# Leads of the projection stream in branch B's three phases raised by 0.2 in a hybrid encoder kernel

## The chip, the cores and the metric

The kernel runs on one core of a Trainium2 chip. The metric is the device time of one execution in microseconds (us); smaller is better. Five engines work beside each other, each through its own instructions in their written order, and wait for each other by semaphores: PE (TensorE, matmuls and transposes, with its weight loads shown apart as PEld), DVE (VectorE), ACT (ScalarE), POOL (GpSimd) and SP (SyncE), which here issues all DMAs.

## The reference, cut to what matters

One encoder layer is applied to two independent groups of 1024 tokens, called prompt (g = 0) and sample (g = 1), with the same weights. From the normalised input `h` one wide projection gives queries, keys and values of two attention branches, their gate paths `z`, and two merge gates `ga`, `gb`.

```
proj = einsum('bsd,de->bse', h, w_in)
qa, ka, va, za, qb, kb, vb, zb, ga, gb = split(proj)
# branch A: 8 query heads on 2 key heads of 64, RMS norm and rotary on q and k
oa = gqa_attention(qa, ka, va) * silu(za)
# branch B: 4 heads; two 64-dim softmax maps per head, 128-dim values
s  = einsum('bqhmd,bkhmd->bhmqk', qblk, k) * scale
p  = softmax(s, axis=-1)
pd = p[:, :, 0] - lam * p[:, :, 1]
ob = rms_norm(einsum('bhqk,bkhe->bqhe', pd, v), subln_g) * (1 - lam_init)
ob = ob * silu(zb)
merged = sigmoid(ga) * (oa @ w_proj_a) + sigmoid(gb) * (ob @ w_proj_b)
y = x + gate * (merged @ w_out)
```

## The kernel before

**Streams of PE work.** Each group is worked off in turn. Within a group there are three kinds of work that compete for PE.

- Attention. `attention` (its steps are sorted by a fixed rule) goes through 32 units: 16 of branch A, then four for each head of branch B. A unit of branch B covers 256 queries and makes four score tiles `s` (128 queries by 1024 keys, one of the two maps). A score tile is four matmuls (L747, L748); DVE takes the row maximum (L749), ACT the exponential (L750). Once both maps of 128 queries are there, DVE joins them with the learned factor that POOL finishes (L775, L776, L790), transposes the result in blocks of 32 (L791), four DMAs put the pieces into place (L800), and about 1.4 units later eight matmuls multiply by the values (L823, tile `a`; the trace records two for each). Score tiles live in two buffers of PSUM (`ps_s`), so a tile can begin only when the exponential of the tile two before it is done.
- Projections for the next head, called here the projection stream. `qkb_gen` makes queries and keys of one head of branch B: for each of eight token tiles 24 matmuls of 256 columns (`proj_tt`, L540), then a chain: two ACT passes (L555, L556), DVE's sum and epsilon (L559, L560), on POOL the power, the norm, the gains and the rotary step (L561, L563, L681, L574, L582, L583, in the tile `row`), and a transpose on PE (L594) two token tiles later, whose result ACT and DVE split into the tiles `u` that the scores read (L596, L597). `vb_gen` makes values for two heads in the same way without the chain.
- Gate pieces. `z_gen` makes the gates `z`, `ga` and `gb`: 24 matmuls of 512 columns for a tile (L713), a tanh, and a DMA to DRAM.

Weights come by DMA into `st`, are split in two parts by ACT (L193) and POOL (L195), and live in two buffers `w` shared by projection stream and gate pieces.

**What sets the order.** `phase(k, ...)` runs phase k of a group: k = 0 and 1 in branch A, k = 2, 3 and 4 for the heads 0, 1 and 2 of branch B, in which the projections for the next head are made (in k = 3 also the values for heads 2 and 3). The last head has no such stream; it is woven with gate pieces and the first steps of the merge. `weave` gives the next turn to the stream whose done share, less its lead, is smallest:

```
s = min(live, key=lambda s: s[2] / s[1] - s[3])
...
n_att = 8 * 6 if k < 2 else 4 * 11
nz = 3 * Z_SHARE[g][k]
weave(
    (until_next(att), n_att * ATT_W[g][k], 0.0), (chain(*fs), 31 * len(fs), IN_A[g][k]),
    (islice(zs, nz), nz, Z_A[g][k]), *more,
)
```

Attention has the lead 0, the projection stream `IN_A[g][k]`, the gate pieces `Z_A[g][k]`. A lead of 0.4 means that the projection stream may be 0.4 of its length ahead of attention. The shares of gate pieces by phase (`Z_SHARE`) are fixed; besides, the end of each `qkb_gen` takes up to two gate steps before each of its last transposes (`pipelined`). The order so written is a wish: a scheduler then orders the instructions of each engine by their priority in the written order and by its own estimate of when each is ready, with attention's instructions raised by 100 places.

Of the kernel before, what the change touches and what calls it, by code (L numbers as in the profile page):

```python
# [44 lines left out]
    (1.229, 1.265, 0.9, 1.0, 0.85, 1.069),  # L45
)
IN_A = (
    (0.1, 0.05, 0.4, 0.05, -0.05, 0.1),
    (0.1, 0.05, 0.4, 0.1, 0.15, 0.55),
)  # L50
Z_A = (
    (0.15, 0.0, 0.2, -0.1, 0.0, 0.0),
# [1284 lines left out]
```

## Time and profile before

| what | value |
|---|---|
| runs before | 1917.95 us median of 3 (1914.27 to 1920.34) |
| the profiled execution's own time | 1911.4 us |
| its span, first to last instruction | 1909.6 us |
| mean granted clock of TensorE | 0.986 |
| DVE busy | 1209.3 us (63%) |
| ACT busy | 771.6 us (40%) |
| POOL busy | 666.6 us (35%) |
| branch B in the prompt group | from about 457 to 790 us |
| branch B in the sample group | from about 1360 to 1710 us |

The profile's page gives busy time by engine, the chain that ended last and the costliest groups of instructions. A window view gives busy time of each engine and the granted clock in stretches that one chooses. A timeline lists instructions in order; in square brackets stands how long the engine sat idle before one and what ended that. Busy time of PE is made from matmuls that overlap in its pipeline: a matmul of 512 columns is recorded with about 0.4 us, while the next one starts about 0.23 us after it.

### The profile page before, as it was taken

To read this page: it belongs to the slowest core of one execution; us is meant where nothing else is said; L and a number is where in the kernel's file an instruction comes from. 1 tells how busy PE (TensorE), PEld (TensorE's weight loads), DVE (VectorE), ACT (ScalarE), POOL (GpSimd) and SP (SyncE) were. 2 spreads that over 40 slices of the span, in tenths; PEclk is the share of its full clock that TensorE was granted. 3 is DMA by queue.
4 is the path that set the end of the run, shared out by engine and by line. 5 is a ranking of instruction groups with operands and counts; after the bars stand their busy time and mean duration, and the time that the engine had idled before them with its cause. 6 is when DMAs were issued, how large, how long until landed. Compare 5 with 4: busy or idle time off the path is not lost.

```text
span 1909.6 us, 29522 instructions
## 1 busy us (share of the span) xinstructions
PE 1847.3 (97%) x10398; PEld 1553.5 (81%) x10398; DVE 1209.3 (63%) x1791; ACT 771.6 (40%) x1576; POOL 666.6 (35%) x904
## 2 busy tenths in 40 slices
PE   6999999999999999999999999999999899999999
PEld 3788778888888978788888877888898798877887
DVE  5777753454876667457467787445366746674795
ACT  4545443443554444213233455344354535332241
POOL 2234511442654551221232343024474736212100
PEclk7999999999999999999999999999999999999999
DMA  9126675554443557864531567665434424586442
GB/s 320 57 84 163 186 199 159 161 151 141 111 123 104 161 152 229 281 183 156 200 107 51 146 188 196 183 182 161 138 92 115 129 70 109 163 254 211 147 126 90
DMA packets 273044, 295.04 MB, mean 155 GB/s; under 512 B 35200, under 2 KB 221696, under 8 KB 272896
## 3 DMA queue, kind: packets, MB, share of 16 engines
q1 hardware_dynamic: 272896, 293.15, 51.8%
q8 instruction: 83, 1.36, 0.3%
q14 instruction: 65, 0.53, 0.1%
HBM read 133.59 MB, written 42.01 MB: 92 GB/s over the span
## 4 chain that ended last, share of the span: by engine, by line
PE 74%; DMA 7%; DVE 6%; SPq 4%; issue 4%; POOL 3%; ACT 2%; DVEq 0%; ACTq 0%; POOLq 0%
PE f L713 20%; PE f L540 17%; PE f L985 5%; PE a L806 5%; PE s L747 5%; PE s L748 5%; PE a L823 4%; PE s L985 3%; PE f L1020 3%; SPq L800 2%; PE s L1020 2%; DMA st<-in_w_in_dram 2%; PE f L1092 2%; DVE m L749 2%; PE s L1092 1%
## 5 line engine op out<-in xcount | busy, mean ns | idle before, releaser
L713 PE MATMUL f<-u,w 128*128 128x512 f32 x2256 | 582.2, 398 | 2.7 <-POOL w L195 1.2
L713 PEld LDWEIGHTS f<-u,w 128*128 128x128 f32 x2256 | 416.5, 189 | 88.9 <-POOL w L195 2.4
L540 PE MATMUL f<-w,u 128*128 128x256 f32 x3456 | 477.8, 287 | 1.3 <-ACT w L193 0.3
L540 PEld LDWEIGHTS f<-w,u 128*128 128x128 f32 x3456 | 452.4, 192 | 22.1 <-issue 3.5
L749 DVE TENSOR_REDUCE m<-s 128x1 f32<-128x1024 f32 x256 | 310.3, 1219 | 200.0 <-PE s L748 198.0
L750 ACT ACTIVATE p<-s,m 128x1024 f32<-128x1024 f32 x256 | 285.1, 1114 | 279.0 <-DVE m L749 238.8
L195 POOL TENSOR_TENSOR w<-st,w 128x512 fp32r<-128x512 f32 x160 | 215.8, 1366 | 441.1 <-ACT w L193 424.8
L791 DVE STREAM_TRANSPOSE p<-p 128x1024 f32<-128x1024 f32 x192 | 237.6, 1241 | 58.0 <-ACT p L750 50.0
L561 POOL TENSOR_TENSOR rs<-ss,nhalf 128x4 f32<-128x4 f32 (+1 forms) x112 | 110.0, 983 | 308.7 <-DVE ss L560 271.8
L748 PE MATMUL s<-u,sw 128*128 128x512 f32 x512 | 203.8, 399 | 0.0
L193 ACT ACTIVATE w<-st 128x512 fp32r<-128x512 f32 x184 | 108.2, 627 | 98.1 <-DMA st<-in_w_in_dram 83.3
L985 PE MATMUL f<-u,w 128*128 128x512 f32 x552 | 134.8, 398 | 2.3 <-DVE u L1000 2.3
L823 PE MATMUL a<-q,u 128*128 128x256 f32 x512 | 127.0, 385 | 8.9 <-DMA q<-p 4.2
L985 PEld LDWEIGHTS f<-u,w 128*128 128x128 f32 x552 | 105.0, 192 | 24.6 <-DVE u L1000 2.5
L597 DVE TENSOR_TENSOR u<-f,u 64x256 fp32r<-64x256 f32 (+1 forms) x194 | 79.7, 411 | 71.3 <-ACT u L596 66.4
L806 PE MATMUL a<-q,u 128*64 128x256 f32 x1024 | 117.8, 382 | 2.0 <-DMA q<-p 2.0
L823 PEld LDWEIGHTS a<-q,u 128*128 128x128 f32 x512 | 95.3, 192 | 24.5 <-issue 7.6
L747 PE MATMUL s<-u 128*128 128x512 f32 x256 | 106.5, 418 | 4.9 <-ACT p L750 4.9
L748 PEld LDWEIGHTS s<-u,sw 128*128 128x128 f32 x512 | 97.2, 190 | 16.8
L790 DVE SCALAR_TENSOR_TENSOR p<-p,r,p 128x1024 f32<-128x1024 f32 x64 | 91.3, 1427 | 28.5 <-POOL r L776 26.8
L806 PEld LDWEIGHTS a<-q,u 128*64 128x64 f32 x1024 | 73.4, 137 | 40.3 <-issue 6.9
L747 PE MATMUL s<-u,u 128*128 128x512 f32 x256 | 102.9, 402 | 1.4 <-ACT p L750 1.4
(215 smaller groups left out, 2032.3 us busy)
## 6 DMA issues: line engine op xcount, KB each, us to landing
q<-p SPq DMA_DIRECT2D x768, 128.0 KB, 2.6
st<-in_w_in_dram SPq DMA_DIRECT2D x132, 256.0 KB, 3.2
zd<-ev SPq DMA_DIRECT2D x96, 256.0 KB, 2.7
sw<-u SPq DMA_DIRECT2D x256, 64.0 KB, 2.0
u<-in_w_ada_dram SPq DMA_DIRECT2D x8, 1024.0 KB, 11.4
od<-oo SPq DMA_DIRECT2D x64, 128.0 KB, 2.4
st<-in_w_in_dram SPq DMA_DIRECT2D x64, 128.0 KB, 2.7
row<-od SPq DMA_DIRECT2D x32, 256.0 KB, 2.9
```

The source lines that it names most:

```text
L195: e.tensor_tensor(out=wl, in0=st, in1=wh.bitcast(F32), op=ALU.subtract)
L540: ins = nc.tensor.matmul(ps, lt[c][:, sl], w[:, c, wi, :], start=(k == 0), stop=(k == 23))
L561: nc.gpsimd.tensor_tensor(out=rs, in0=ss, in1=nhalf[:, :nh], op=ALU.pow)
L713: ins = nc.tensor.matmul(ps, w[:, c, wi, e * P : (e + 1) * P], rt[c], start=(k == 0), stop=(k == 23),)
L747: nc.tensor.matmul(s[:, sl], q, k[:, sl], start=True, stop=False)
L748: nc.tensor.matmul(s[:, sl], sw, k[:, sl], start=False, stop=True)
L749: nc.vector.tensor_reduce(out=m, in_=s, axis=AX.X, op=ALU.max, negate=True)
L750: nc.scalar.activation(pt.rearrange("p (j c a) -> p j c a", j=4, c=8), s.rearrange("p (c a j) -> p j c a", c=8, j=4), AF.Exp, bias=m, accu ...
L791: nc.vector.transpose(pt, pt)
L806: lambda k=k, m=m: nc.tensor.matmul(acc[(LO, HI)[m]], u["v"][:, k], pT[m][:, k], start=(k == 0), stop=(k == 7))
L823: nc.tensor.matmul(acc, u["v"][:, k], pT[:, k], start=(k == 0), stop=(k == 7))
L985: nc.tensor.matmul(ps, w[:, c, wi, d * P : (d + 1) * P], o[:, oi, :], start=(k == 0), stop=(k == 11))
```

## The change

Six numbers of one table change: the lead of the projection stream in phases 2, 3 and 4 of each group goes up by 0.2. In both groups phase 2 goes from 0.4 to 0.6; phases 3 and 4 go from 0.05 and -0.05 to 0.25 and 0.15 in the prompt group, and from 0.1 and 0.15 to 0.3 and 0.35 in the sample group. No instruction is added or taken away; their order on all five engines differs from the beginning of phase 2 to the end of branch B in each group, and nowhere else.

```diff
 IN_A = (
-    (0.1, 0.05, 0.4, 0.05, -0.05, 0.1),
-    (0.1, 0.05, 0.4, 0.1, 0.15, 0.55),
+    (0.1, 0.05, 0.6, 0.25, 0.15, 0.1),
+    (0.1, 0.05, 0.6, 0.3, 0.35, 0.55),
 )
```

Three places show what becomes of it on PE.

**Place 1**, PE at the end of phase 4 of the prompt group, before: `a_7241` are the values of the last unit of head 2, `f_7103` a gate tile, `f_7192` and `f_7251` a side computation of the residual's gate (L325), `s_7185` and `s_7208` the first score tiles of head 3, `f_7114` and `f_7151` the last two transposes of its queries and keys.

```order
L594 MATMUL f_7114<-ident,row_6954 128x128 x2
L713 MATMUL f_7103<-u_329,w_7086 128x512
L713 MATMUL f_7103<-u_330,w_7086 128x512
L713 MATMUL f_7103<-u_329,w_7086 128x512 x2
L713 MATMUL f_7103<-u_330,w_7086 128x512
L713 MATMUL f_7103<-u_329,w_7086 128x512
L823 MATMUL a_7241<-q_7066,u_5989 128x256 x8
L594 MATMUL f_7151<-ident,row_7025 128x128 x2
L325 MATMUL f_7192<-u_7193,cT 32x512 x4
L835 MATMUL f_7221<-ones_c,at_7196 128x1 x2
L325 MATMUL f_7192<-u_7218,cT 32x512 x4
```

The same place on PE in the changed kernel; the last transposes and the gate tile stand ahead of these rows.

```order
L325 MATMUL f_7192<-u_7193,cT 32x512 x4
L325 MATMUL f_7192<-u_7218,cT 32x512 x4
L835 MATMUL f_7221<-ones_c,at_7196 128x1 x2
L747 MATMUL s_7185<-u_6425 128x512
L748 MATMUL s_7185<-u_6425,sw_7141 128x512
L747 MATMUL s_7208<-u_6426 128x512
L748 MATMUL s_7208<-u_6426,sw_7141 128x512
L337 MATMUL f_7244<-pick,row_7242 128x2 x4
L325 MATMUL f_7251<-u_7252,cT 32x512 x4
L325 MATMUL f_7251<-u_7272,cT 32x512 x4
L823 MATMUL a_7241<-q_7136,u_5909 128x256 x8
```

The values `a_7241` moved behind both L325 tiles, the last transposes and the second halves of two score tiles; ahead of it, 21 matmuls of the projection stream that stood after the unit's last score tile are gone, since the stream ended earlier.

**Place 2**, PE at the end of phase 2 of the sample group, before: the last token tile of head 1's queries and keys is transposed into `f_14163`, with the scores of `s_14428`, the first tile of head 1, ahead of it.

```order
L713 MATMUL f_14100<-u_9082,w_13524 128x512
L747 MATMUL s_14293<-u_12421 128x512
L748 MATMUL s_14293<-u_12421,sw_14181 128x512
L747 MATMUL s_14293<-u_12421 128x512
L748 MATMUL s_14293<-u_12421,sw_14181 128x512
L747 MATMUL s_14428<-u_13503 128x512
L748 MATMUL s_14428<-u_13503,sw_14271 128x512
L594 MATMUL f_14163<-ident,row_14066 128x128
```

In the changed kernel the same token tile is transposed into `f_14099`.

```order
L747 MATMUL s_14279<-u_12420 128x512
L748 MATMUL s_14279<-u_12420,sw_14181 128x512
L713 MATMUL f_14071<-u_9082,w_13604 128x512
L713 MATMUL f_14071<-u_9084,w_13604 128x512
L713 MATMUL f_14071<-u_9082,w_13604 128x512 x2
L713 MATMUL f_14071<-u_9084,w_13604 128x512
L713 MATMUL f_14071<-u_9082,w_13604 128x512
L594 MATMUL f_14099<-ident,row_13972 128x128
```

Between the last projection matmul of this token tile and its transpose there stood 30 gate matmuls and 14 score matmuls; now 42 gate matmuls, 16 score matmuls and the eight of a unit's values stand there.

**Place 3**, PE at the end of phase 3 of the sample group, before: three score tiles of head 1 in a row (a fourth, `s_15151`, stands just ahead of them), then a transpose of the projection stream and a gate tile.

```order
L747 MATMUL s_15239<-u_13503 128x512
L748 MATMUL s_15239<-u_13503,sw_15117 128x512
L747 MATMUL s_15239<-u_13503 128x512
L748 MATMUL s_15239<-u_13503,sw_15117 128x512
L747 MATMUL s_15254<-u_13504 128x512
L748 MATMUL s_15254<-u_13504,sw_15117 128x512
L747 MATMUL s_15254<-u_13504 128x512
L748 MATMUL s_15254<-u_13504,sw_15117 128x512
L594 MATMUL f_14824<-ident,row_14707 128x128 x2
L713 MATMUL f_14848<-u_9077,w_14831 128x512
```

The same place on PE in the changed kernel.

```order
L594 MATMUL f_14734<-ident,row_14582 128x128 x2
L823 MATMUL a_15026<-q_14703,u_11710 128x256 x8
L747 MATMUL s_15217<-u_13504 128x512
L748 MATMUL s_15217<-u_13504,sw_15011 128x512
L747 MATMUL s_15217<-u_13504 128x512
L748 MATMUL s_15217<-u_13504,sw_15011 128x512
L747 MATMUL s_15239<-u_13503 128x512
L748 MATMUL s_15239<-u_13503,sw_15195 128x512
L747 MATMUL s_15239<-u_13503 128x512
L748 MATMUL s_15239<-u_13503,sw_15195 128x512
L594 MATMUL f_14761<-ident,row_14638 128x128 x2
L713 MATMUL f_14785<-u_9077,w_14768 128x512
```

The run of four score tiles is broken up: a unit's values stand ahead of `s_15217`, and a transpose and 22 gate matmuls now stand between `s_15239` and `s_15254`.

## The prediction

> **What bounds the kernel now.** The page comes first: its opening line and its first list show which engine has no room.
>
> ```profile
> span 1909.6 us, 29522 instructions
> PE 1847.3 (97%) x10398; PEld 1553.5 (81%) x10398; DVE 1209.3 (63%) x1791; ACT 771.6 (40%) x1576; POOL 666.6 (35%) x904
> ```
>
> PE is busy for 97% of the span, and the change neither adds nor removes a matmul. A gain can only come out of PE's gaps, and a loss only from new ones. So the second view is the busy time by stretch, here the three projection phases and the last head, first of the prompt group, then of the sample group. The columns are stretch, length, busy time of PE, PEld, DVE, ACT and POOL with counts, granted clock, DMA share, GB/s.
>
> ```profile
> 470.00:530.00 60.00, 59.95 (x343) 51.99 (x340) 44.61 (x62) 32.05 (x68) 35.75 (x59) 1.00 0.37 102
> 530.00:600.00 70.00, 68.50 (x420) 61.39 (x420) 51.99 (x76) 34.70 (x75) 41.66 (x74) 1.00 0.42 117
> 600.00:682.00 82.00, 82.00 (x539) 75.55 (x538) 55.95 (x79) 37.88 (x80) 41.04 (x62) 1.00 0.51 147
> 682.00:790.00 108.00, 101.43 (x487) 81.66 (x486) 69.72 (x99) 41.26 (x78) 31.29 (x42) 0.98 0.69 212
> 1385.00:1446.00 61.00, 61.00 (x369) 54.52 (x368) 44.78 (x63) 32.34 (x67) 41.08 (x65) 1.00 0.39 105
> 1446.00:1514.00 68.00, 59.71 (x354) 51.94 (x352) 48.27 (x74) 34.66 (x74) 43.95 (x73) 0.95 0.41 112
> 1514.00:1590.00 76.00, 76.00 (x508) 70.55 (x507) 39.62 (x60) 28.11 (x60) 30.18 (x50) 1.00 0.33 91
> 1590.00:1710.00 120.00, 116.57 (x552) 97.93 (x552) 82.14 (x107) 53.65 (x102) 44.56 (x61) 0.99 0.61 180
> ```
>
> Three of the eight rows have no gap at all, a fourth has 0.05 us. What there is to win lies in three rows: 1.50, 6.57 and 8.29 us of idle PE, with the clock below 1.00 in the last two; of the 6.57, place 1 holds 3.44, and the rest stands with the final row's 3.43 in the last heads, where the order hardly changes. The third view, PE's timeline, gives each long gap and what ended it.
>
> ```profile
> 695.84 5.38 PE L823 MATMUL a<-q,u 128*128 128x256 f32 x16 [3.44 <-DMA q<-p]
> 1450.02 0.33 PE L594 MATMUL f<-ident,row 128*128 128x128 f32 x1 [2.62 <-POOL row L583]
> 1450.62 5.73 PE L713 MATMUL f<-u,w 128*128 128x512 f32 x17
> 1508.50 0.50 PE L747 MATMUL s<-u 128*128 128x512 f32 x1 [2.84 <-ACT p L750]
> 1510.42 0.63 PE L748 MATMUL s<-u,sw 128*128 128x512 f32 x1
> 1510.85 0.63 PE L747 MATMUL s<-u 128*128 128x512 f32 x1
> 1513.78 0.44 PE L594 MATMUL f<-ident,row 128*128 128x128 f32 x2 [1.88 <-POOL row L583]
> 589.73 3.61 PE L823 MATMUL a<-q,u 128*128 128x256 f32 x16
> 600.84 4.02 PE L713 MATMUL f<-u,w 128*128 128x512 f32 x17
> ```
>
> Four gaps, and behind three of them slow work: the same 16 matmuls took 5.38 us instead of 3.61, the same 17 took 5.73 instead of 4.02, and score matmuls of the same width began 0.43 us apart instead of 0.24 (4.02 / 17). So a long gap costs its length and about 1.7 us more: **3.44 + 1.77 = 5.2** (place 1), **2.62 + 1.71 = 4.3** (place 2), **2.84 + 1.88 + 8 x 0.19 = 6.2** (place 3). Together 15.7 us stand on what ends each phase: the next head's last transposes, or scores and values packed together.
>
> [...]
>
> **The change, part by part.** No instruction is new, so the terms are waits that go, waits that stay, and waits that come.
>
> *Place 1, goes nearly: -5.2 + 1.0.* The values must wait for the last score tile of their unit, its softmax and four DMAs.
>
> ```profile
> 682.70 0.39 PE L748 MATMUL s<-u,sw 128*128 128x512 f32 x1
> 683.43 1.23 DVE L749 TENSOR_REDUCE m<-s 128x1 f32<-128x1024 f32 x1
> 690.95 1.93 SPq L800 DMA_DIRECT2D q<-p  x3
> 701.36 1.07 PE L325 MATMUL f<-u,cT 128*32 128x512 f32 x8
> ```
>
> From the last score matmul's end (683.09) to the values (695.84) the need is 12.7 us. In the changed order these stand between them: 24 gate matmuls, 24 x 0.236 = 5.7 (4.02 / 17); 8 score matmuls, 1.9; the L325 tiles, four times 1.07 = 4.3; two transposes and small ones, about 1.2. That is 13.1, so the wait is just covered. It is covered by little: SP, where a load for L325 and one for `st` stand ahead of the last pieces `q`, can add delay, and the 1.07 may hold some of the half clock. Bounds for what stays are 0 and 5.2; I take 1.0, near the cover worked out.
>
> *Place 2, goes: -4.3.* The transpose waited for POOL's rotary step, and POOL for a weight split that stood between the norm and the gains of this token tile.
>
> ```profile
> 1437.02 0.39 ACT L555 ACTIVATE row<-f 128x256 f32<-128x256 f32 x1
> 1443.13 1.02 POOL L561 TENSOR_TENSOR rs<-ss,nhalf 128x4 f32<-128x4 f32 x1 [1.31 <-DVE r L775]
> 1444.44 0.61 POOL L563 TENSOR_TENSOR row<-row,rs 128x256 f32<-128x256 f32 x1
> 1446.80 1.28 POOL L195 TENSOR_TENSOR w<-st,w 128x512 fp32r<-128x512 f32 x1 [1.74 <-ACT w L193]
> 1448.03 0.73 POOL L681 TENSOR_TENSOR row<-row,gB 128x256 f32<-128x256 f32 x1
> 1449.11 0.46 POOL L582 TENSOR_TENSOR row<-row,sinB 128x32 f32<-128x32 f32 x2
> 1449.65 0.32 POOL L583 TENSOR_TENSOR row<-rc,row 128x64 f32<-128x64 f32 x1
> ```
>
> The chain took 12.95 us (1437.02 to 1449.97) against 44 matmuls of cover, some 10.4 us. The changed order has 42 x 0.236 + 16 x 0.24 + 3.6 for the values = 17.3 us of cover, 4.4 more than the chain needed. If a weight piece came that much later the wait would be back; bounds 0 and 4.3, taken as gone.
>
> *Place 3, halves: -6.2 + 3.1.* Here DVE is the slower engine for a while. Its rows from 1458 to 1515, with one stretch, and 24 projection matmuls of the chain of waits:
>
> ```profile
> L749 DVE TENSOR_REDUCE m<-s 128x1 f32<-128x1024 f32 x14 | 17.1, 1219 | 5.2 <-PE s L748 5.1
> L790 DVE SCALAR_TENSOR_TENSOR p<-p,r,p 128x1024 f32<-128x1024 f32 x6 | 8.1, 1342 | 1.4 <-POOL r L776 1.4
> L791 DVE STREAM_TRANSPOSE p<-p 128x1024 f32<-128x1024 f32 x5 | 6.2, 1240 | 0.1
> L597 DVE TENSOR_TENSOR u<-f,u 64x256 fp32r<-64x256 f32 x12 | 5.1, 422 | 1.1 <-ACT u L596 0.9
> L559 DVE TENSOR_REDUCE ss<-row 128x4 f32<-128x256 f32 x8 | 3.3, 410 | 0.9 <-ACT row L556 0.8
> 1500.00:1515.00 15.00, 10.21 (x54) 7.79 (x53) 14.10 (x20) 10.63 (x22) 13.34 (x21) 0.89 0.46 123
> 657.68 2.87 PE f L540 x24
> ```
>
> DVE worked 14.10 of 15 us at the two gaps. In the changed order the four tiles no longer stand together, but a stretch ahead of them is denser: over eight score tiles (up to `s_15217`) DVE has 8 maxima (9.8), 4 joins (5.4), 4 transposes (5.0), 8 splits (3.4), 4 sums (1.6) and about 2.2 of small work, 27.4 us; PE has 32 score matmuls (7.6), 72 projection matmuls (8.6, at 2.87 for 24), 8 for values (3.6) and about 0.9 of small ones, 20.7 us. The difference of 6.7 us is spread over eight tiles, each of which may run up to one tile late for nothing, since there are two score buffers. Bounds are 0 (all hidden) and 6.7 + 1.7 = 8.4 (all shown in one piece); I take half the old cost, 3.1.
>
> *Small waits, stay and come: +2.0.* The remaining gaps between 470 and 1515 are of this size:
>
> ```profile
> PE f L713 <- DVE ssB L837: 1.0, 1, 1.0
> PE f L594 <- POOL row L583: 0.5, 1, 0.5
> 1485.00:1500.00 15.00, 14.12 (x91) 12.61 (x90) 10.73 (x19) 8.92 (x20) 10.79 (x20) 1.00 0.52 142
> ```
>
> The first two are from the list of who waited for whom, the third is a stretch with 0.88 us idle. I leave these as they are, and add two new ones of 1.0 for bursts: in the changed order most phases begin with some 72 projection matmuls close together, so three token tiles reach POOL at once. Bounds are 0 and three waits like place 2, 13. At nothing I cost the gate pieces' new places (PE's total is the same), the earlier weight loads (their buffers come free 5 us or more of PE work ahead, as before), and SP's shifts in the last head; their cover is PE's own backlog.
>
> **Sum**: -5.2 + 1.0 - 4.3 - 6.2 + 3.1 + 2.0 = **-9.6 us**. On the profiled execution's own 1911.4 us that gives 1901.8. Its own time lies 6.5 us below the median of the runs, 1917.95; the gain is taken off the median: **1908.3 us**.
>
> **Rivals.**
>
> *DVE takes it back.* At place 3 all of the 8.4 us shows, 5.3 more than taken: -4.3, 1913.7. For it speaks DVE's 14.10 of 15; against it that before, the tiles stood closer. [...] Chance 0.22.
>
> *POOL becomes the bound, slower.* Three token tiles in a burst of 8.6 us bring POOL 3 x (1.02 + 0.61 + 0.73 + 0.46 + 0.32) = 9.4 us and a little for the cosine step, beside four weight splits of 1.28, so about 15. If the transposes, 10 to 12 us behind in PE's order, wait as at place 2 in most of the six phases, each costs 4.3. From the third such wait on, the gain is used up (3 x 4.3 = 12.9 against 11.6 without the 2.0); six make 25.8 - 11.6 = +14.2, 1932. Against it: POOL is busy for 41 of 61 us and less elsewhere, and the cover of the last transpose grew where it had waited. Chance 0.10.
>
> *All waits of these phases go*, the small ones too: -15.7 - 1.0 - 0.5 - 0.9 = -18.1, 1899.9. Chance 0.10.
>
> *It does not do what it says.* The ends of the phases were full already: the rows 600:682 and 1514:1590 have PE at 100%, so gates put there fill nothing, and the four gaps are chance meetings that reappear elsewhere at the same price. 1918. Against it: each of the three places has its own longer cover in the new order. Chance 0.08.
>
> **How the numbers follow.** Forecast 0.50, the rivals 0.22, 0.10, 0.10, 0.08. About 0.3% (5.75 us) is what a measurement of this kernel can tell from no change, so faster is below 1912.2. The forecast falls below it but for 0.05, the greater gain wholly, and 0.05 of the first rival: faster 0.45 + 0.10 + 0.05 = 0.60. Within: 0.05 + 0.17 + 0.08 = 0.30; slower 0.10. The range goes from 1897, a little under the case in which all goes, to 1921, which takes in no change and part of the slower side; it leaves out the upper part of the POOL case and a tail of the others.
>
> **What would show it.** Right: no PE gap over 2 us before the values at the end of the prompt's phase 4, none before the last transpose of the sample's phase 2, granted clock 1.00 in both; at the sample's phase 3 a few gaps of about 1 us ended by ACT. Wrong: gaps of PE ended by POOL L583 early in the phases (the slower rival), or several us ended by ACT L750 at the sample's phase 3 (the first). The forecast fails if the waits move rather than go: the same 8 and 6 us in other rows of the stretch table.

## The result, and the profile after

The kernel was compared with the one before twice; the second comparison is run e9 below.

| comparison | before | after | ratio, 95% interval |
|---|---|---|---|
| first, 5 runs and 5 | 1917.75 us (1914.27 to 1920.34) | 1905.77 us (1902.43 to 1909.83) | 0.9940 [0.9920, 0.9961] |
| second, 23 runs and 10 | 1913.41 us (1905.84 to 1923.92) | 1905.24 us (1900.65 to 1907.85) | 0.9963 [0.9949, 0.9976] |

The changed kernel is faster by 12.0 or 8.2 us. The two medians of the changed kernel agree within 0.5 us; the kernel before differs by 4.3. The profiled execution after is the run of 1905.77, against 1911.4 for that of before: between the two traces the difference is 5.6 us.

The page's first lines, as before: the same matmuls, the same busy time of PE.

```profile
span 1904.0 us, 29515 instructions
PE 1846.8 (97%) x10398; PEld 1554.6 (82%) x10398; DVE 1212.2 (64%) x1791; ACT 771.7 (41%) x1576; POOL 666.1 (35%) x904
```

Busy time by stretch, the same columns and the same eight stretches of work. Their bounds moved with the work, so the lengths differ from those before.

```profile
470.00:530.00 60.00, 60.00 (x334) 51.89 (x331) 45.18 (x64) 33.29 (x69) 36.39 (x61) 1.00 0.41 115
530.00:600.00 70.00, 68.02 (x415) 61.14 (x414) 51.53 (x75) 33.83 (x72) 39.80 (x71) 0.98 0.41 112
600.00:692.00 92.00, 91.12 (x583) 82.86 (x583) 57.99 (x83) 41.99 (x89) 50.75 (x77) 1.00 0.47 135
692.00:790.00 98.00, 94.70 (x453) 75.84 (x452) 68.06 (x91) 37.26 (x70) 23.73 (x30) 1.00 0.78 240
1385.00:1446.00 61.00, 60.22 (x361) 53.30 (x359) 47.64 (x68) 32.80 (x71) 43.54 (x71) 1.00 0.41 114
1446.00:1506.00 60.00, 55.33 (x337) 49.56 (x336) 44.54 (x66) 30.42 (x65) 42.19 (x67) 0.97 0.42 115
1506.00:1582.00 76.00, 76.00 (x511) 70.50 (x510) 44.01 (x65) 31.70 (x67) 30.53 (x56) 1.00 0.34 90
1582.00:1705.00 123.00, 118.73 (x551) 98.95 (x550) 81.83 (x105) 52.11 (x99) 42.93 (x54) 0.97 0.59 178
```

The fourth row lost 3.3 us of idle time (6.57 to 3.30): the 3.44 of place 1 go, 1.47 come (at 696.97), and the last head's own waits are 1.3 shorter. The sixth row still has 4.67 us of its 8.29: place 2 is gone, place 3 is not. PE's timeline of the changed kernel, only the rows in front of which PE sat idle in the projection phases (the row at 684.23 also shows what 16 matmuls for values take at full clock: 3.69 us, granted clock 1.00 from 684.25 to 687.90), and ahead of the last one the end of the values of the unit before it:

```profile
590.22 0.44 PE L594 MATMUL f<-ident,row 128*128 128x128 f32 x2 [1.21 <-POOL row L583]
591.30 0.67 PE L594 MATMUL f<-ident,row 128*128 128x128 f32 x2 [0.65 <-POOL row L583]
670.57 3.26 PE L823 MATMUL a<-q,u 128*128 128x256 f32 x14 [0.23 <-DMA q<-p]
684.23 3.69 PE L823 MATMUL a<-q,u 128*128 128x256 f32 x16 [0.51 <-DVE r L775]
696.97 0.33 PE L594 MATMUL f<-ident,row 128*128 128x128 f32 x1 [1.47 <-POOL row L583]
1417.74 3.69 PE L823 MATMUL a<-q,u 128*128 128x256 f32 x16 [0.78 <-DMA sw<-u]
1473.15 1.46 PE L823 MATMUL a<-q,u 128*128 128x256 f32 x6
1499.18 5.41 PE L823 MATMUL a<-q,u 128*128 128x256 f32 x16 [4.62 <-DVE oo L829]
```

The last row is the one to look at. At the end of the sample's phase 3 the values wait 4.62 us and then run 1.72 us longer than the 16 of another unit do at 684.23 (5.41 us instead of 3.69; granted clock 0.50 from 1499.35 to 1502.70), 6.3 us together. What they wait for is the copy L829, which empties the only accumulator `a` (the pool `ps_a` has one buffer). DVE's rows at that place:

```profile
1495.17 1.22 DVE L749 TENSOR_REDUCE m<-s 128x1 f32<-128x1024 f32 x1
1496.43 2.03 DVE L790 SCALAR_TENSOR_TENSOR p<-p,r,p 128x1024 f32<-128x1024 f32 x1
1498.38 0.41 DVE L559 TENSOR_REDUCE ss<-row 128x4 f32<-128x256 f32 x1
1498.71 0.41 DVE L829 COPY oo<-a 128x256 f32<-128x256 f32 x1
```

DVE has no pause in them. The copy stands in its queue behind a maximum, a join and a sum, so PE waits for work that has nothing to do with the accumulator. PE stopped at 1494.56. Of the 4.62 us from there, 0.61 pass before DVE begins the maximum of the tile that PE has just finished, 1.26 go with that maximum, 1.95 with the join, 0.33 with the sum and 0.47 with the copy. The values that the copy takes out had ended at 1474.61 already, 24.1 us before the copy began; ACT's square of the same accumulator (L828), which stands just as late in ACT's order, ran at 1495.14.

### The profile page after: what moved, and what is told of

It reads as the page before. It is cut to its first block, busy times and chain, and to the rows that moved or that the text cites. A ratio compares the mean times of both kernels' runs of the same rounds, so it can differ in the third digit from the quotient of the medians.

```text
span 1904.0 us, 29515 instructions
## 1 busy us (share of the span) xinstructions
PE 1846.8 (97%) x10398; PEld 1554.6 (82%) x10398; DVE 1212.2 (64%) x1791; ACT 771.7 (41%) x1576; POOL 666.1 (35%) x904
## 4 chain that ended last, share of the span: by engine, by line
PE 70%; DMA 8%; DVE 7%; POOL 5%; issue 4%; SPq 3%; ACT 2%; POOLq 0%; DVEq 0%; ACTq 0%
PE f L713 18%; PE f L540 16%; PE a L806 5%; PE f L985 5%; PE s L747 4%; PE s L748 4%; PE a L823 3%; PE s L985 3%; PE f L1020 3%; DMA row<-zd 2%; SPq L800 2%; PE s L1020 2%; DVE m L749 2%; PE f L1092 2%; DMA q<-p 1%
## 5 line engine op out<-in xcount | busy, mean ns | idle before, releaser
L540 PE MATMUL f<-w,u 128*128 128x256 f32 x3456 | 470.9, 287 | 1.7 <-ACT w L193 0.9
L750 ACT ACTIVATE p<-s,m 128x1024 f32<-128x1024 f32 x256 | 285.1, 1114 | 290.6 <-DVE m L749 227.8
L790 DVE SCALAR_TENSOR_TENSOR p<-p,r,p 128x1024 f32<-128x1024 f32 x64 | 89.2, 1393 | 20.6 <-POOL r L776 18.7
## 6 DMA issues: line engine op xcount, KB each, us to landing
u<-in_w_ada_dram SPq DMA_DIRECT2D x8, 1024.0 KB, 11.4
```

The source lines that it names most:

```text
L540: ins = nc.tensor.matmul(ps, lt[c][:, sl], w[:, c, wi, :], start=(k == 0), stop=(k == 23))
L750: nc.scalar.activation(pt.rearrange("p (j c a) -> p j c a", j=4, c=8), s.rearrange("p (c a j) -> p j c a", c=8, j=4), AF.Exp, bias=m, accu ...
```

## The experiments

Two questions were open: does each place win on its own, so that a larger lead is a dial to turn (theory A), or do the waits only meet by chance in each order (theory B)? And is the wait at place 3 one of DVE's load? "PE idle" below is 490 us less PE's busy time in the windows 455 to 705 and 1360 to 1600 us, which hold the projection phases; it was 13.27 us before and is 9.78 after. Each ratio is against runs of the kernel before on the same chip. PE idle is that of the one execution that was profiled; in e3, e6 and e8 it took 1913.02, 1912.79 and 1920.29 us, 6 to 9 us away from the median.

| run | leads raised by | median, us | ratio, 95% interval | PE idle, us |
|---|---|---|---|---|
| e1 | 0.2, prompt only | 1907.54 | 0.9969 [0.9957, 0.9982] | 12.27 |
| e2 | 0.2, sample only | 1908.85 | 0.9977 [0.9964, 0.9990] | 11.90 |
| e3 | 0.1 | 1920.40 | 1.0043 [1.0029, 1.0058] | 17.51 |
| e4 | 0.4 | 1934.36 | 1.0113 [1.0092, 1.0133] | 23.21 |
| e5 | 0.02 | 1930.93 | 1.0101 [1.0083, 1.0119] | 24.13 |
| e6 | 0.22 | 1906.84 | 0.9977 [0.9962, 0.9993] | 11.17 |
| e7 | 0.2, not in the sample's phase 3 | 1907.34 | 0.9980 [0.9968, 0.9992] | 14.20 |
| e8 | 0.2, copy L829 on ACT | 1911.76 | 0.9995 [0.9978, 1.0012] | 17.15 |
| e9 | 0.2, the changed kernel again | 1905.24 | 0.9963 [0.9949, 0.9976] | 10.06 |
| e10 | 0.2, joins and transposes cut | 1887.18 | 0.9860 [0.9839, 0.9882] | 3.30 |
| e11 | 0.4, joins and transposes cut | 1920.31 | 1.0038 [1.0023, 1.0052] | 18.48 |
| e12 | 0.02, joins and transposes cut | 1908.40 | 0.9969 [0.9954, 0.9984] | 14.48 |

### One group at a time (e1, e2), and the whole once more (e9)

```diff
 IN_A = (
-    (0.1, 0.05, 0.4, 0.05, -0.05, 0.1),
+    (0.1, 0.05, 0.6, 0.25, 0.15, 0.1),
     (0.1, 0.05, 0.4, 0.1, 0.15, 0.55),
 )
```

That is e1; e2 changes the second row alone, e9 both.

> Only the prompt group's three leads are raised; the sample group keeps the order of before. Theory A, each place has its own cover: the wait for the values at the prompt's phase 4 (place 1) goes and nothing else changes, so the gain is what the traces show up to the start of the sample group, 3.6 to 3.8 us, about 1914 against a kernel before of 1917.8; its PE gaps in the sample group are those of before, with 2.62 us ahead of the last transpose of phase 2 and 2.84 us among the score tiles of phase 3. Theory B, chance meetings: the gain is not tied to the group; it lies anywhere from 0 to 12 us, and gaps in the sample group differ from before although the order there is the same.

> Only the sample group's three leads are raised. Theory A: place 2 is won (4.3 us) and place 3 is not (a gap of 4 to 5 us ahead of the values that wait for the copy L829 on DVE, and the half clock behind it), so 1917.8 - 4.3 = 1913.5, and this gain and that of the prompt group alone add up to the whole one, 8 us by this count and 12 by the medians. Theory B: the gap of 4 to 5 us at place 3 is not there or is of another size, and the two gains don't add up to within 4 us.

> The changed kernel once more, beside the three that follow. Theory A, the parts add up: the prompt group alone gave a ratio of 0.9969 and the sample group alone 0.9977, so the whole should give 0.9946, which is also near its first 0.994; with a kernel before of 1912 to 1914, as in the two earlier comparisons, that is 1902 to 1904. Rival: the first 0.994 was helped by a slow draw of the kernel before (five runs, 1917.75), and the whole is worth less than its parts, about 0.997.

PE's timeline of e1 in the sample group, whose order it leaves as it was (rows with a wait over 1 us):

```profile
1445.89 0.33 PE L594 MATMUL f<-ident,row 128*128 128x128 f32 x1 [2.55 <-POOL row L583]
1504.31 0.50 PE L747 MATMUL s<-u 128*128 128x512 f32 x1 [2.85 <-ACT p L750]
1509.27 0.69 PE L594 MATMUL f<-ident,row 128*128 128x128 f32 x2 [1.89 <-POOL row L583]
```

And that of e2, at place 1 (whose order it leaves) and at place 3:

```profile
697.25 3.17 PE L823 MATMUL a<-q,u 128*128 128x256 f32 x8 [3.87 <-DMA st<-in_w_in_dram]
1502.20 5.98 PE L823 MATMUL a<-q,u 128*128 128x256 f32 x16 [4.63 <-DVE oo L829]
```

e1 has the gaps of before at places 2 and 3 (2.62, 2.84 and 1.88 there) to within 0.1 us; e2 has place 1 still (3.87 us where 3.44 stood before, put down to another transfer) and the changed kernel's 4.62 to within 0.01. So for a given order the waits are nearly fixed, and they belong to their place: in this theory A held. Whether the two gains add up in full is less sure. The ratios multiply to 0.9946; the first comparison's interval takes that in, e9's (from 0.9949) just leaves it out, and e9's 0.9963 lies nearer its rival's 0.997 than theory A's 0.9946. So the first 0.9940 probably owes something to its base, 1917.75 us, against 1911.71 to 1914.06 in the three later comparisons. The gains of 6.5 and 5.2 us by medians, against 1914.06, are larger than the 3.7 and 4.3 expected from single traces, but their intervals reach down to 3.4 and 1.9.

### The lead as a dial (e3, e4, e5, e6)

```diff
-    (0.1, 0.05, 0.4, 0.05, -0.05, 0.1),
-    (0.1, 0.05, 0.4, 0.1, 0.15, 0.55),
+    (0.1, 0.05, 0.42, 0.07, -0.03, 0.1),
+    (0.1, 0.05, 0.42, 0.12, 0.17, 0.55),
```

This is e5; the others raise the same six numbers by 0.1, 0.4 and 0.22.

> All six leads are raised by 0.1 and not by 0.2. Theory A, the cover grows with the lead: a gain between none and the whole, 1905.8 to 1917.8, with places 1 and 2 shorter than 3.44 and 2.62 us or gone. Theory B, chance meetings: the time may lie outside these two, by up to 10 us on either side, with gaps at places where neither kernel has them.

> All six leads are raised by 0.4. Theory A, cover: places 1 and 2 stay gone; the time is within 4 us of the changed kernel, 1902 to 1910, unless POOL becomes the bound in the denser bursts at the phases' beginnings, which would show as PE gaps ended by POOL L583 there, 4.3 us each. Theory B, chance meetings: the time lies outside 1902 to 1910, with long gaps that are ended by other things than POOL L583.

> The kernel before with all six leads raised by 0.02. Theory A, cover: a lead of 0.02 hardly moves what stands between a producer and its consumer, so the long gaps of before stay and the time is within 3 us of 1917.8. Theory B, chance meetings: another order of a few instructions changes which waits meet, and the time moves by as much as the whole change did, 5 to 12 us either way.

> The changed kernel with all six leads raised by 0.02 more. Theory A: within 3 us of 1905.8, places 1 and 2 without a long gap. Theory B: 5 to 12 us from it either way, with long gaps at places where the changed kernel has none or without the 4.62 us at place 3.

0.02 costs 1%, 0.1 costs 0.4%, 0.2 gains 0.4 to 0.6%, 0.22 gains 0.2%, 0.4 costs 1.1%. The lead is no dial; here theory B held, but for e6, which stays close to the changed kernel in time with other gaps (2.3 us ended by POOL in the sample group's phases in place of the 4.62). The lists of who waited for whom say what took the time: engine and line that waited, what ended it, us in total, times, longest. In e5, from 455 to 705 (two rows) and then from 1360 to 1600, POOL and ACT alone:

```profile
PE f L594 <- POOL row L583: 7.1, 2, 4.2
PE s L747 <- ACT p L750: 3.4, 2, 1.8
PE s L747 <- ACT p L750: 8.0, 6, 2.3
PE f L594 <- POOL row L583: 2.9, 2, 1.6
```

The longest, 4.2 us, stands at the end of the prompt's phase 4, where the kernel before waited for values. POOL's timeline ahead of that transpose:

```profile
694.15 1.02 POOL L561 TENSOR_TENSOR rs<-ss,nhalf 128x4 f32<-128x4 f32 x1 [4.78 <-DVE ss L560]
...
698.83 0.46 POOL L582 TENSOR_TENSOR row<-row,sinB 128x32 f32<-128x32 f32 x2
699.24 0.20 POOL L840 TENSOR_TENSOR suB<-suB 128x8 f32<-128x8 f32 x1
699.40 2.49 POOL L195 TENSOR_TENSOR w<-st,w 128x512 fp32r<-128x512 f32 x2
701.85 0.61 POOL L563 TENSOR_TENSOR row<-row,rs 128x256 f32<-128x256 f32 x1
702.42 1.26 POOL L195 TENSOR_TENSOR w<-st,w 128x512 fp32r<-128x512 f32 x1
703.64 0.31 POOL L583 TENSOR_TENSOR row<-rc,row 128x64 f32<-128x64 f32 x1
```

Three weight splits and another token tile's norm stand between the last two steps of this one, 4.35 us: place 2's pattern, at another place. Ahead of it POOL had also waited 4.78 us for DVE. So what a lead changes is not only the cover but which weight piece, which score tile and which copy fall together at the phases' ends, and that follows no order of leads.

### Place 3 by its lead and by its copy (e7, e8)

e7 is the changed kernel with the sample's phase 3 left at 0.1. e8 moves the copy:

```diff
-        nc.vector.tensor_copy(query_order(o), piece_order(acc))
+        nc.scalar.activation(query_order(o), piece_order(acc), AF.Copy)
```

> The changed kernel, but the sample group's phase 3 keeps its lead of 0.1. If the changed order of that phase is what brought the gap of 4.62 us ahead of the values (4.62 and about 1.8 us of slow clock, 6.4), that gap goes and the four packed score tiles come back at 6.2 us: within 2 us of 1905.8. If the wait at place 3 belongs to the old order alone and the new order was to halve it, this is 3 us slower than the changed kernel, 1909. If the phases' ends are chance, neither gap need appear, and the time may fall by 6 us, 1899.

> The changed kernel with the copy L829, which frees the only accumulator `a` of the values, on ACT instead of DVE. Theory C, the copy's place in DVE's queue: the values at place 3 no longer wait behind the maxima and a join on DVE, and the gap of 4.62 us with the slow clock behind it goes, 6.4 us less, 1899.4; ACT's 64 copies of about 0.4 us (26 us over the kernel) are hidden, since ACT is busy for 41% of the span. Theory D, DVE's load: the score tiles run late by what DVE is behind, and the wait comes back as gaps ended by ACT p L750 of 2 to 4 us at place 3, so the time is within 3 us of 1905.8. Theory E: ACT's exponentials come later by 0.4 us at each copy, the score tiles wait for them, and it is slower than 1910.

In e7 the copy's wait is gone and three waits for `p` stand there (2.31, 2.69 and 2.14 us, at 1502, 1508 and 1511), more than before had; with 1907.34 us that is the first of the three outcomes. Its ratio of 0.9980 and e9's 0.9963 overlap, so which of the two orders of phase 3 is better stays open; neither avoids the wait.

In e8 the wait for the accumulator falls from 4.62 to 1.30 us, now ended by ACT, and the 16 matmuls behind it take 3.72 us, as theory C has it for this wait. But PE waits 5.26 us for ACT p L750 a little later (until 1523.62; the values began at 1512.42). That is theory D's picture with a longer gap, and the time theory E's (1911.76, over 1910): the interval takes in no change against before. (The expectation counted 64 copies; branch B has 32, so 13 us.) But the scheduler also ordered everything anew, so e8 doesn't show that the copy's place alone did it. The last three runs therefore keep the order.

### DVE lighter, the order kept (e10, e11, e12)

After scheduling, the two instructions of branch B's joins and transposes are replaced by the same ones on 32 columns; the work on the other 992 is left out, while order and semaphores stay.

```diff
-            nc.vector.scalar_tensor_tensor(out=pt, in0=p1, scalar=f, in1=pt, op0=ALU.mult, op1=ALU.add)
-        nc.vector.transpose(pt, pt)
+            cheap.append(nc.vector.scalar_tensor_tensor(out=pt, in0=p1, scalar=f, in1=pt, op0=ALU.mult, op1=ALU.add))
+        (cheap if 'h' in u else []).append(nc.vector.transpose(pt, pt))
...
+    few = lambda a: a.__replace__(ap=[a.ap[0], [1, 32]]) if len(a.ap) > 1 and a.ap[-1][1] == 1024 else a
+    names = {x.ins.name for x in cheap}
+    for block in nc.m.functions[0].blocks:
+        block.instructions = [
+            i.__replace__(ins=tuple(few(a) for a in i.ins), outs=tuple(few(a) for a in i.outs))
+            if i.name in names else i
+            for i in block.instructions
+        ]
```

> The changed kernel with the order of all engines kept as it is, in which the 64 joins L790 and the 64 block transposes L791 of branch B do 32 of their 1024 columns; the rest of each is left out. That takes some 1.15 us off each, 147 us of DVE's 1212. Theory D, DVE's backlog: the gap of 4.62 us at place 3 has two parts. The copy L829 stands behind the maximum of the tile that PE has just finished, which leaves 2.0 to 2.5 us; the rest, 2.1 to 2.6 us, is backlog and goes. Waits of PE ended by ACT p L750 in branch B go too; together 5 to 9 us less than the changed kernel. Rival: the wait belongs to the order alone, the gap stays over 4 us and the time within 2 us of the changed kernel.

> The kernel with leads raised by 0.4, order kept, with the same joins and transposes cut to 32 columns. Theory D: what the larger lead costs (1.0113 of the kernel before; in its trace 21.9 us of PE gaps ended by ACT p L750 in the phases, where score tiles stand packed with nothing of the projection stream left between them) is DVE's backlog; these gaps fall below 6 us and the time by 15 to 25 us, so it is within 5 us of the changed kernel cut in the same way. Rival: the score buffers' turn (maximum, exponential, next tile) sets these gaps by itself; more than half of the 21.9 us stays.

> The kernel with leads raised by 0.02, order kept, with the same joins and transposes cut to 32 columns. Its trace has, in the phases, 13.4 us of PE gaps ended by ACT p L750 and 10.6 us ended by POOL L583, against 4.1 and 5.7 in the kernel before. Theory D: the first go with DVE's load, the second stay unless POOL's chain was waiting for DVE's sums; the time falls by 8 to 15 us from 1931, not to the changed kernel's. Rival: the nudge's loss lies in other things (POOL, weights, slow clock) and the time falls by less than 6 us.

**e10.** Place 3 again, PE's timeline and then DVE's:

```profile
1486.63 5.41 PE L823 MATMUL a<-q,u 128*128 128x256 f32 x16 [2.52 <-DVE oo L829]
```

```profile
1482.56 1.23 DVE L749 TENSOR_REDUCE m<-s 128x1 f32<-128x1024 f32 x1 [1.20 <-PE s L748]
...
1484.34 1.23 DVE L749 TENSOR_REDUCE m<-s 128x1 f32<-128x1024 f32 x1
1485.60 0.32 DVE L790 SCALAR_TENSOR_TENSOR p<-p,r,p 128x32 f32<-128x32 f32 x1
1485.84 0.41 DVE L559 TENSOR_REDUCE ss<-row 128x4 f32<-128x256 f32 x1
1486.17 0.41 DVE L829 COPY oo<-a 128x256 f32<-128x256 f32 x1
```

The wait is 2.52 us, as theory D's sizes had it, but not for theory D's reason. DVE now waits for PE ahead of these rows (1.20 us), so it has no backlog. It begins the last maximum 0.23 us after PE stops (at 1484.11) instead of 0.61, and from the join's start to the sum's pass 0.24 us instead of 1.95. So of the 2.1 us that went, only 0.4 were backlog; 1.7 are the length of the join itself, which this run cuts. The copy still begins 21.6 us after its values ended (at 1464.60), although DVE has idle time in between. The wait is thus mainly one of order: PE stands behind the copy, and the copy behind the maximum of a tile that PE has only just finished. No run moves the copy alone with the rest of the order kept.

The whole fell by 18.1 us against e9, not by 5 to 9: PE is idle for 3.30 us instead of 10.06. The order is the same, so the two traces (17.0 us apart) can be compared matmul by matmul. In the work that e9 does in the two windows e10 gains 12.1 us, and 9.3 in the rest of the two last heads, whose joins are cut too and which theory D hadn't counted; elsewhere it loses a few us. In the windows, waits ended by POOL L583 (3.9 us in e9 from 455 to 705) are gone as well.

**e11 and e12.** The lists of who waited for whom, e11, from 455 to 705 and from 1360 to 1600 (e4 had 8.0 and 11.6 us here):

```profile
PE s L747 <- ACT p L750: 5.0, 5, 2.3
PE s L747 <- ACT p L750: 11.2, 6, 3.2
```

The same for e12:

```profile
PE s L747 <- ACT p L750: 3.3, 3, 1.5
PE f L594 <- POOL row L583: 2.7, 2, 2.2
PE s L747 <- ACT p L750: 6.5, 5, 2.0
PE f L594 <- POOL row L583: 1.7, 2, 1.4
```

Against theory D, the waits for `p` stay for the most part (19.6 to 16.2 us in e11, 11.4 to 9.8 in e12), and the rival's sign, more than half stays, is what came. What falls with DVE's load is the wait for POOL, from 10.0 to 4.4 us in e12, whose time falls by 22.5 us, more than either theory had. The rival's reason, that the turn of the two score buffers sets these waits by itself, is not shown: ACT's timeline of e11 ahead of its longest gap (3.23 us, PE waiting from 1510 to 1513.42) shows one more thing that stands in the way:

```profile
1510.08 0.38 ACT L555 ACTIVATE row<-f 128x256 f32<-128x256 f32 x1 [2.44 <-PE f L540]
1510.36 1.66 ACT L193 ACTIVATE w<-st 128x512 fp32r<-128x512 f32 x3
1511.92 0.36 ACT L596 ACTIVATE u<-f 64x256 fp32r<-64x256 f32 x1
1512.18 1.10 ACT L750 ACTIVATE p<-s,m 128x1024 f32<-128x1024 f32 x1
```

The exponential that PE waits for is queued behind a projection's copy, which waited 2.44 us for PE itself, and behind three weight splits. Its maximum was done by 1508.56 at the latest. e11 as a whole fell by 14.0 us, a little less than theory D's 15, and stays 33 us above e10, where theory D had 5.

## Why the prediction came near in time and was wrong in a step

| step | predicted, us | measured between the two traces, us |
|---|---|---|
| place 1 | -5.2 + 1.0 | -5.2 + 1.5 (the transpose at 696.97) |
| place 2 | -4.3 | -4.3 |
| place 3 | -6.2 + 3.1 | -6.2 + 6.3 (4.62 + 1.72) |
| small waits | +2.0 | +2.4: 1.0, 0.5 and 0.88 go; 1.21, 0.65, 0.23, 0.51 and 0.78 come, and 1.4 of slow clock |
| sum | -9.6 | -5.5; the traces differ by 5.6, the medians by 8.2 and 12.0 |

The measured terms add up to what the two traces differ by, but by group they do so less well. Where the order is the same again behind branch B, the changed kernel's trace has gained 2.9 us over the prompt's branch B and 2.4 over the sample's; the terms give 1.2 and 4.3. The rest, about 1.8 us each way, fits the last heads, where the prediction had put nothing: their idle PE beside place 1 falls from 3.13 to 1.83 us in the prompt group and rises from 3.43 to 4.27 in the sample group, with the clock there at 0.97 instead of 0.99. That it cancels is luck.

**Place 1 held.** The values no longer wait. What stays is not what was named (SP's queue): the last transpose now waits for POOL's chain. In e9, the same program, the longest of the three waits for POOL L583 between 455 and 705 us was 2.1 us, and the clock granted from 692 to 790 us was 0.98 instead of 1.00, so more than 1.5 us can stay there.

**Place 2 held** as worked out: no wait in front of the last transpose of the sample's phase 2, in the changed kernel, e2 and e9.

**Place 3 is the step that failed.** "The four tiles no longer stand together" was true, and the gaps at score tiles went: DVE's maxima there began up to 2.2 us after their tiles, and PE lost nothing by it. But the halving took it that a delay of DVE shows at score tiles alone, "spread over eight tiles, each of which may run up to one tile late for nothing, since there are two score buffers". The values stand among those tiles, and their accumulator has one buffer, whose release is an instruction late in DVE's order. So the term +3.1 measured 6.3, in one piece. It is what the rival "DVE takes it back" feared, but by another instruction than it named (L829, not ACT L750), at 6.3 us in place of 8.4, and by another cause: not the load that DVE is behind by, of which e10 took away 0.4 us, but what stands ahead of the copy in its queue.

**The small waits** came at POOL L583 as expected, and in the changed kernel's trace they stayed small. The slower rival, POOL as the bound, is no fancy: leads of 0.02 and 0.1 show it, with gaps of 4.20 us (e5) and 5.32 us (e3) at the end of the prompt's phase 4. It is not POOL's own work alone: with DVE's work cut more than half of these waits goes (10.0 to 4.4 us, e12).

**"It does not do what it says"** was too cheaply put aside. The places keep their covers, as was argued, and e1 and e2 show it; but a neighbouring order builds new meetings at the same price, and at the other leads these came with the loss.

**The base** was too high: the median of three runs, 1917.95, against 1911.71 to 1914.06 in three later comparisons with 23 to 29 runs of the kernel before. A sum of -9.6, a little more than e9's -8.2, on a base 4.5 us above 1913.41 gave 1908.3, 3 us above what was measured. Two errors against each other brought it that near, which is luck. e9's interval, a gain of 4.6 to 9.8 us, takes in both the predicted 9.6 and the traces' 5.6, so the times alone don't tell which sum is right; that place 3 was wrong is read from the traces.

**The half clock.** The prediction charged 1.7 us for each long gap. In the two windows of the traces before and after, the granted clock fell to 0.50 for 3.4 us each time: before from 696.6, 1451.0 and 1509.0, after from 591.4 and 1499.3. Half of 3.4 is the 1.7 charged. PE's timelines of twelve runs, before and after among them, show 16 gaps of 2.5 us or more there, from 2.52 us (e10) to 5.32 us (e3). All 16 were followed by slow clock: 16 matmuls for values took 5.38 to 6.29 us instead of 3.61 to 3.69, or score matmuls began 0.43 us apart instead of 0.23. Behind shorter gaps it came in some cases (1.21 and 0.65 us at 590.22 and 591.30 of the changed kernel) and not in others (1.47 us at 696.97, granted clock 1.00 from 695.5 to 700), and not the same in each run (last section).

## What to carry to other kernels

Where an order's small change is to fill gaps, look at every buffer that exists only once, and at what stands ahead of the instruction that frees it in its engine's order; a wait can gather there even where that engine has time to spare (2.52 us in e10, where DVE itself had waited 1.20 us for PE). Test the neighbours of a tuned number before reading its size as a cause: here 0.02 moved the time by 1%, more than the change itself. And cut an instruction's size after scheduling, with the order kept, to learn what an engine's load costs, and read row by row whether a wait fell because the engine was less behind or because the cut instruction stood in the way. With DVE's joins and transposes cut, PE's idle time in the two windows fell by two thirds in the changed order, by 40% with the lead raised by 0.02 and by 20% with 0.4, so the answer holds for one order only.

## What was not expected of the hardware

**The same gap costs 1.4 us in one run and nothing in another.** The changed kernel and e1 are the same program up to the sample group. Both wait 1.2 and 0.65 us for POOL in front of the same transposes. PE's timeline right behind, first of the changed kernel, then of e1:

```profile
591.63 4.49 PE L540 MATMUL f<-w,u 128*128 128x256 f32 x24
```

```profile
591.53 3.11 PE L540 MATMUL f<-w,u 128*128 128x256 f32 x24
```

24 matmuls take 4.49 us in one, with a granted clock of 0.50 from 591.40 to 594.75, and 3.11 in the other. In e9, the changed kernel once more, the clock granted from 530 to 600 us was 1.00, against 0.98 in the changed kernel's first trace. Some of the scatter of a few us between runs of one kernel can come from this. What decides between the two prices, no run shows. Where the slow clock came, 1.9 us in two pieces (1.21 and 0.65, here) or 2.52 us in one (e10) were enough.

**Some joins on DVE and some passes on POOL took longer beside each other.** With no POOL instruction beside it, each of 22 joins L790 took 1.28 to 1.29 us in the changed kernel's trace; with one beside it up to 2.27, though half of those 42 took no longer. Groups of instructions from 455 to 705 us, POOL's in e9 and then in e10 (busy us and mean ns behind the bar):

```profile
L195 POOL TENSOR_TENSOR w<-st,w 128x512 fp32r<-128x512 f32 x28 | 38.3, 1387 | 51.3 <-ACT w L193 51.2
L681 POOL TENSOR_TENSOR row<-row,gB 128x256 f32<-128x256 f32 x24 | 22.3, 930 | 1.2
```

```profile
L195 POOL TENSOR_TENSOR w<-st,w 128x512 fp32r<-128x512 f32 x28 | 35.5, 1289 | 54.2 <-ACT w L193 54.2
L681 POOL TENSOR_TENSOR row<-row,gB 128x256 f32<-128x256 f32 x24 | 17.6, 736 | 1.2
```

The same 24 gains took 930 ns on average beside full joins and 736 beside cut ones. What makes them longer, no run shows. How much of e10's 18 us comes by this, and how much by DVE's sums being ready earlier for POOL, no run separates.
